# Layer 1's adaLN blocks summed in the scan and the output projection instead of in the MLPs and the q, k projections

## The chip, the cores and the metric

The kernel runs on one core of one Trainium2 chip. The metric is the device time of one execution in microseconds; the time quoted is the median of three executions.

## The reference, cut to what matters

Two layers are applied to 512 latent and 128 context tokens of width 1024. Layer 0 mixes tokens with a bidirectional RWKV-7 scan, layer 1 with neighbourhood attention; each is followed by a squared-ReLU MLP. Each layer has six adaLN vectors (shift, scale and gate, twice), and they depend on the conditioning vectors and on weights alone, not on the tokens:

```python
def ada_mod(cond, w, b):
    m = jax.nn.silu(cond) @ w + b
    return jnp.split(m, 6, axis=-1)

for l in range(DEPTH):            # for the context tokens with c_ctx, for the latent ones with c
    sh1, sc1, gt1, sh2, sc2, gt2 = ada_mod(c, ada_w[l], ada_b[l])
    h = modulate(rms_norm(xs, norm_g[l, 0]), sh1, sc1)
    o = mixer(h, ...)             # l = 0: rwkv7_mixer, l = 1: na_latent / na_context
    xs = xs + gt1[:, None, :] * o
    h = modulate(rms_norm(xs, norm_g[l, 1]), sh2, sc2)
    xs = xs + gt2[:, None, :] * sq_relu_mlp(h, mlp_w1[l], mlp_w2[l])
```

So layer 1's vectors may be made at any time before layer 1 begins, and the later ones up to their use.

## The kernel before, in words

**An adaLN block.** The 6144 columns of one layer's `ada_w` are cut in 24 blocks of 256 columns, 1 MB each. `ada_first` (L279) loads a block as two halves of 512 KB into two buffers of the name `adaraw`, issued on SP, sums it with eight matmuls (16 instructions in the trace) and copies the sum to `adasb` on ACT. `ada_second` (L292) turns the sum over with two small matmuls (4 instructions) and adds the bias on DVE (L300) into `mods`. The pool `adp` has two `adaraw` buffers, so a block's loads wait until the matmuls of the block before have read theirs.

**Where the 48 blocks were summed.** Layer 0's first eight are summed in `start_norm`, its other sixteen in the scan, one a turn. Layer 1's 24 are summed by `ada_later` (L1275), which also takes one block: eight inside MLP 0, twelve inside the q and k projections of `phase_na`, four inside the first quarter of MLP 1.

**The scan.** `phase_scan` (L753) goes through five steps n = 0 to 4, each with four turns e = 0 to 3; (n, e) names a turn. A turn takes one chunk of 32 tokens in either direction: `chain_step` (L981) runs as the generators s0 (direction d = 0) and s1 (d = 1). Each does a state product (`A<-GU,C`), a copy of it on ACT (`Rc`), a solve with the step's inverse (`A<-Rc,TT`), a scaled copy back on ACT (`GU`, L1032), a state update (`B<-GU,C`), and an output product (`A<-GU,C` again). Between these, `fill` (L863) puts the matmuls (`pp<-C,KB`) that prepare the next step, and `invert` (L959) computes the next step's inverse by a long row of small DVE instructions (L973, L976), ending in `TT` (L978). `ada_next` (L777) puts one adaLN block after the first of the turn's fills. The small matmuls of `ada_second` write columns 256 to 259 of the PSUM tile that holds the solve of d = 1, in the same bank. Finished tiles go through `post_half` (L1094), on DVE and GpSimd.

**What sets the order.** While `self.pin` is set, `mm` (L830) chains the scan's matmuls so that TensorE runs them in program order; each other engine has an order laid down when the kernel is built. SP issues nearly all loads, in its own order.

**After the scan.** `wo_first` (L1162) does the output projection for 384 of the 640 tokens. Its weights (L1169) and its inputs `ol` (L1181, L1182) are loaded into the same two `adaraw` buffers, after the last adaLN block. `phase_wo` (L1204) does the other 256 tokens, in eight blocks k with one 512 KB weight block each. Then MLP 0, `phase_na` and MLP 1 follow, whose products are the matmuls of L205.

Of the kernel before, what the change touches and what calls it, by code (L numbers as in the profile page):

```python
# [14 lines left out]
PSUM = bass.MemoryType.PSUM  # L15
# [157 lines left out]
class K:  # L173
# [237 lines left out]
    def rest_begin(self, st):  # L411
        self.sqp = self.pool(st, "sqp", 2)
        self.ada1 = list(range(24))

    def pool(self, st, name, bufs, **k):
        return st.enter_context(self.tc.tile_pool(name=name, bufs=bufs, reuse_waits="tile", **k))
# [336 lines left out]
    def phase_scan(self, st):  # L753
        nc, tc = self.nc, self.tc
        if True:
            pool = lambda name, bufs, **k: self.pool(st, name, bufs, **k)
            self.yp = pool("yp", 4)
            adp = pool("adp", 2)
# [15 lines left out]
            todo, running = [], []  # L774
            ada = [(0, b) for b in range(8, 24)]

# [11 lines left out]
            for n, ts in enumerate(self.steps):  # L788
                for e in range(4):
                    s0, s1 = (self.chain_step(ts, n, e, d) for d in range(2))  # L790
                    next(s0)
                    if pend:
                        for x in pend:
                            next(x)
                        if n == 4 and not self.late:
                            self.late_pools()
                        for t in done.get((n, e - 1) if e else (n - 1, 3), []):
                            todo.append(self.post_half(*t, n == 4 and t[0] % 3))
# [26 lines left out]
            for _ in range(3):  # L825
                for x in todo:
                    next(x)
            self.wo_first(adp)

# [151 lines left out]
    def chain_step(self, ts, n, e, d):  # L981
# [38 lines left out]
        for ph, pp, hp in idx:  # L1020
# [4 lines left out]
                    rhs=Rc[qs, o], start=True, stop=True, tile_position=(32 * q, 32 * q))  # L1025
        if self.ada_sums and d == 1:
            self.ada_second(*self.ada_sums.pop(0), ut[:, 256:260], self.mm)
# [176 lines left out]
    def phase_wo(self):  # L1204

        nc, tc = self.nc, self.tc
        with ExitStack() as st:
            pool = lambda name, bufs, **k: self.pool(st, name, bufs, **k)
            self.wraw = pool("wraw", 4, side="right")
            self.whl = pool("whl", 3, side="right")  # L1210
            self.psl = pool("psl", 4, space=PSUM)
            xp = pool("xp", 8)
# [14 lines left out]
            for k in range(8):  # L1227
# [3 lines left out]
                nc.gpsimd.tensor_copy(self.x[:, k, TS:], xa[:, 256:])  # L1231
                w = self.wblock(self.A["w_o"][k])
                ps = self.psl.tile([P, 512], F32, name="psl")[:, :256]
                for f in range(8):
# [333 lines left out]
```

## Time and profile before

| | |
|---|---|
| median of three executions | 2248.33 us (2247.55 to 2261.33) |
| the profiled execution's own time | 2250.36 us |
| its span, first to last instruction | 2248.5 us |
| TensorE busy | 2007.7 us, 89% |
| VectorE (DVE) busy | 1180.0 us, 52% |
| ScalarE (ACT) busy | 866.0 us, 39% |
| GpSimd (POOL) busy | 463.8 us, 21% |
| scan, by the trace | about 410 to 798 us |
| rest of the output projection | about 798 to 886 us |
| MLP 0, attention layer, MLP 1 | about 886 us to the end |

The shares are means over stages with different limits, so each stage has to be read by itself. Times of the trace count from the span's start. PE is TensorE's matmul, SP the engine that issues most loads. A row in square brackets at a line's end gives the idle time before it and what ended it.

### The profile page before, as it was taken

The page shows a single profiled execution, that of the slowest core. Times are in us where ns is not written, and L with a number is a line of the kernel's source. Part 1 is how long each engine was busy: PE and PEld are TensorE (multiplying, and loading weights), DVE is VectorE, ACT ScalarE, POOL GpSimd, SP SyncE. Part 2 cuts the span into 40 slices and gives each one's busy share as a digit, 9 for nine tenths or more (in the row PEclk, how much of TensorE's full clock was granted, in tenths as well). Part 3 has the DMA queues.
Part 4 walks back from the last instruction along what each step waited for, and adds up shares of the span by engine and source line. Part 5 has one row for each costly group of instructions (what it writes and reads, how often), then busy time and mean ns, then how long its engine had stood idle before and what let it go on. Part 6 is the DMA issues. An engine that isn't in the chain of part 4 may idle for free.

```text
span 2248.5 us, 44838 instructions
## 1 busy us (share of the span) xinstructions
PE 2007.7 (89%) x18516; PEld 1823.6 (81%) x18516; DVE 1180.0 (52%) x2587; ACT 866.0 (39%) x1735; POOL 463.8 (21%) x558
## 2 busy tenths in 40 slices
PE   5898978757665677999999999999999999999999
PEld 3787877646554566999999998888777999999999
DVE  6847667396687766433333334434566643434342
ACT  3544554356553425413131323221576331313130
POOL 0001257566552323101010110000232210101010
PEclk9897989888888798999999999999899999999999
DMA  6454864444443455323232223433311232222221
GB/s 232 123 154 140 251 204 158 141 149 148 131 130 121 101 181 164 94 75 113 76 104 75 94 75 114 137 116 108 111 58 29 75 123 75 75 76 74 74 75 70
DMA packets 161388, 260.01 MB, mean 116 GB/s; under 512 B 46880, under 2 KB 103328, under 8 KB 161184
## 3 DMA queue, kind: packets, MB, share of 16 engines
q1 hardware_dynamic: 146816, 240.37, 34.2%
q10 hardware_dynamic: 14368, 16.78, 2.3%
q8 instruction: 145, 2.38, 0.4%
q14 instruction: 59, 0.48, 0.1%
HBM read 218.18 MB, written 37.35 MB: 114 GB/s over the span
## 4 chain that ended last, share of the span: by engine, by line
PE 73%; DVE 13%; DMA 6%; ACT 3%; POOL 2%; issue 2%; SPq 1%; ACTq 0%; DVEq 0%; POOLq 0%
PE psl L205 53%; PE psl L239 4%; PE ps L1495 2%; DVE invT L973 2%; DVE invX L976 2%; PE po L1532 2%; PE pp L832 2%; POOL C L927 2%; PE pt L1520 2%; DVE C L957 1%; PE psl L286 1%; DMA ld_s<-scr 1%; PE pp L1199 1%; DMA wi<-scr 1%; PE st L548 1%
## 5 line engine op out<-in xcount | busy, mean ns | idle before, releaser
L191 ACT CAST whi<-wraw 128x1024 fp32r<-128x1024 f32 x179 | 187.2, 1048 | 730.9 <-PE psl L205 702.5
L205 PE MATMUL psl<-xh,whi 128*128 128x320 f32 (+1 forms) x1712 | 419.8, 318 | 20.8 <-ACT whi L191 15.1
L205 PE MATMUL psl<-xl,whi 128*128 128x320 f32 (+1 forms) x1712 | 417.0, 316 | 7.9 <-DVE xl L248 7.9
L205 PE MATMUL psl<-xh,wlo 128*128 128x320 f32 (+1 forms) x1712 | 415.0, 315 | 2.6 <-DVE wlo L193 2.6
L205 PEld LDWEIGHTS psl<-xh,whi 128*128 128x128 f32 x1712 | 295.4, 192 | 39.4 <-ACT whi L191 19.3
L205 PEld LDWEIGHTS psl<-xl,whi 128*128 128x128 f32 x1712 | 296.3, 192 | 13.9 <-DVE xl L248 10.0
L205 PEld LDWEIGHTS psl<-xh,wlo 128*128 128x128 f32 x1712 | 297.1, 192 | 5.2 <-DVE wlo L193 3.0
L1152 DVE SCALAR_TENSOR_TENSOR xres<-psl,mods,xres 128x320 f32<-128x320 f32 (+2 forms) x216 | 81.7, 434 | 305.5 <-PE psl L205 305.5
L1315 POOL TENSOR_TENSOR relu<-relu 128x640 f32<-128x640 f32 x64 | 80.8, 1263 | 753.1 <-ACT relu L1314 736.2
L205 PE MATMUL psl<-hhh,wlo 128*128 128x320 f32 x1024 | 233.5, 309 | 0.0
L205 PE MATMUL psl<-hhh,whi 128*128 128x320 f32 x1024 | 233.2, 309 | 0.0
L205 PE MATMUL psl<-hhl,whi 128*128 128x320 f32 x1024 | 233.2, 309 | 0.0
L193 DVE TENSOR_TENSOR wlo<-wraw,whi 128x1024 fp32r<-128x1024 f32 x179 | 222.5, 1245 | 14.2 <-ACT whi L191 14.0
L205 PEld LDWEIGHTS psl<-hhh,whi 128*128 128x128 f32 x1024 | 171.2, 188 | 0.4 <-issue 0.4
L205 PEld LDWEIGHTS psl<-hhl,whi 128*128 128x128 f32 x1024 | 171.1, 188 | 0.0
L205 PEld LDWEIGHTS psl<-hhh,wlo 128*128 128x128 f32 x1024 | 171.1, 188 | 0.0
L1272 DVE TENSOR_TENSOR relu<-psl,rms_b 128x320 f32<-128x320 f32 x128 | 60.7, 486 | 144.4 <-PE psl L205 143.3
L832 PE MATMUL pp<-C,KB 128*64 128x128 f32 x1280 | 97.6, 298 | 27.2 <-DVE C L957 13.1
L248 DVE TENSOR_TENSOR hhl<-relu,hhh 128x640 fp32r<-128x640 f32 x64 | 53.4, 834 | 127.9 <-ACT hhh L247 127.8
L832 PEld LDWEIGHTS pp<-C,KB 128*64 128x64 f32 x1280 | 79.9, 149 | 41.3 <-issue 20.7
L957 DVE TENSOR_TENSOR C<-pp,cstsb 64x512 f32<-64x512 f32 x80 | 55.1, 689 | 76.5 <-ACT C L954 68.9
L1032 ACT ACTIVATE GU<-A 32x256 f32<-32x256 f32 x160 | 60.0, 375 | 84.3 <-DVE mods L300 51.8
(288 smaller groups left out, 3389.7 us busy)
## 6 DMA issues: line engine op xcount, KB each, us to landing
wraw<-in_mlp_w SPq DMA_DIRECT2D x128, 512.0 KB, 3.5
adaraw<-in_ada_w SPq DMA_DIRECT2D x96, 512.0 KB, 4.9
ld_d<-scr SPq DMA_DIRECT2D x20, 512.0 KB, 4.1
ld_s<-scr SPq DMA_DIRECT2D x20, 512.0 KB, 3.9
bias<-in_bias SPq DMA_DIRECT2D x16, 384.0 KB, 3.5
scr<-ta SPq DMA_DIRECT2D x16, 325.0 KB, 3.5
wi<-scr SPq DMA_DIRECT2D x20, 260.0 KB, 4.5
scr<-bp SPq DMA_DIRECT2D x16, 320.0 KB, 4.6
```

Source lines behind the costliest of these rows:

```text
L191: nc.scalar.copy(hi, raw)
L193: nc.vector.tensor_tensor(lo, raw, hi.bitcast(F32), op=ALU.subtract)
L205: self.nc.tensor.matmul(ps[g][:, :e - c], lhsT=a[:, k, :], rhs=b[:, c:e], start=(k == 0 and j == 0), stop=(k == n - 1 and j == 2))
L239: nc.tensor.matmul(ps, lhsT=a[:, tc_], rhs=w, start=(k == 0 and j == 0), stop=(k == KT - 1 and j == 2))
L248: (lo_eng or nc.vector).tensor_tensor(xl, src, xh.bitcast(F32), op=ALU.subtract)
L832: r = (op or self.nc.tensor.matmul)(*a, **k)
L927: nc.gpsimd.tensor_tensor(rev(o) if s == 0 else o, v4(sh, s, ww)[hs], f[hs], op=ALU.mult)
L957: nc.vector.tensor_tensor(C[o, 8 * h:8 * h + 8, :], pn[o, :, 0:64], mask[o], op=ALU.mult)
L1032: nc.scalar.activation(gu[64 - 64 * hp:96 - 64 * hp, hp, pp].rearrange("p b v -> p (b v)"), U[32 * q:32 * q + 32, :], AF.Copy, scale=-0.5)
L1152: nc.vector.scalar_tensor_tensor(out[:, a:b], ps[g][:, o:o + b - a], gate[:, k, j:j + 1], x[:, a:b], op0=ALU.mult, op1=ALU.add)
L1272: nc.vector.tensor_tensor(t[:, c], ps[q][:, :HALF], rb[:, c], op=ALU.mult)
L1315: nc.gpsimd.tensor_tensor(t, t, t, op=ALU.mult)
```

## The change

The list of layer 1's blocks is made at the start of the scan and appended to the scan's own list, so that this list has 40 blocks. A second block is taken in each turn of step 0, and in the turns e = 0, 2 and 3 of the later steps; it stands right after the first state product of d = 0. `ada_second` is done in either direction's solve tile, no longer in that of d = 1 alone. The scan's 36 places take 16 blocks of layer 0 and 20 of layer 1; `phase_wo` gets a pool `adp` of its own and a fifth PSUM buffer, and sums the last four blocks in its first four turns k. The calls of `ada_later` in the MLPs and in the projections find the list empty and do nothing.

```diff
     def rest_begin(self, st):
         self.sqp = self.pool(st, "sqp", 2)
-        self.ada1 = list(range(24))
...
     def phase_scan(self, st):
         nc, tc = self.nc, self.tc
+        self.ada1 = list(range(24))
...
-            ada = [(0, b) for b in range(8, 24)]
+            ada = [(0, b) for b in range(8, 24)] + [(1, b) for b in self.ada1]
...
                     next(s0)
+                    if n == 0 or e != 1:
+                        ada_next()
                     if pend:
...
                 for x in todo:
                     next(x)
+            self.ada1 = [b for _, b in ada]
             self.wo_first(adp)
...
-        if self.ada_sums and d == 1:
+        if self.ada_sums:
             self.ada_second(*self.ada_sums.pop(0), ut[:, 256:260], self.mm)
...
-            self.psl = pool("psl", 4, space=PSUM)
+            self.psl = pool("psl", 5, space=PSUM)
+            self.adp = pool("adp", 2)
...
                 w = self.wblock(self.A["w_o"][k])
+                self.ada_later()
```

## Rows read from the trace of the kernel before

**Rows 1.** The page's busy times: us, share of the span, instructions.
```profile
PE 2007.7 (89%) x18516; PEld 1823.6 (81%) x18516; DVE 1180.0 (52%) x2587; ACT 866.0 (39%) x1735; POOL 463.8 (21%) x558
```

**Rows 2.** Chain of waits in MLP 0 and the k projection: start, us, engine, tile, line.
```profile
1023.85 1.00 PE psl L286 x16
1029.18 0.34 PE psl L296 x4
...
1395.24 0.54 PE psl L296 x4
...
1399.83 1.00 PE psl L286 x16
```

**Rows 3.** Busy time by stage: window, length, engines, clock, DMA share, GB/s.
```profile
454.00:508.00 54.00, 26.51 (x708) 21.38 (x699) 52.94 (x141) 26.83 (x66) 31.88 (x47) 0.78 0.47 145
508.00:536.00 28.00, 26.35 (x692) 20.73 (x692) 9.65 (x22) 18.95 (x51) 15.48 (x22) 0.94 0.44 139
...
737.00:770.00 33.00, 21.48 (x679) 18.11 (x670) 28.43 (x73) 12.84 (x31) 3.37 (x3) 0.81 0.45 111
...
798.00:843.00 45.00, 34.10 (x211) 31.88 (x209) 31.50 (x66) 10.08 (x12) 8.01 (x5) 0.96 0.66 201
843.00:890.00 47.00, 32.03 (x207) 30.64 (x208) 32.69 (x49) 28.26 (x63) 18.68 (x22) 0.82 0.51 160
...
1024.00:1130.00 106.00, 106.00 (x742) 104.70 (x735) 39.07 (x69) 28.06 (x38) 8.79 (x7) 1.00 0.28 92
```

**Rows 4.** Waits in the scan: who waited for whom, us in total, times, longest.
```profile
ACT GU L1032 <- DVE mods L300: 51.8, 16, 13.0
...
SPq L284 <- PE pp L832: 45.7, 16, 13.5
```

**Rows 5.** Timeline of PE, DVE and ACT at the end of turn (3, 3).
```profile
719.72 0.61 PE L832 MATMUL A<-cstsb,adasb 128*128 128x2 f32 x4
...
731.40 0.15 DVE L300 TENSOR_TENSOR mods<-A,parsb 128x4 f32<-128x4 f32 x1
...
731.59 1.57 ACT L1032 ACTIVATE GU<-A 32x256 f32<-32x256 f32 x4 [13.02 <-DVE mods L300]
```

**Rows 6.** Timeline of PE in turns (0, 0) and (0, 1).
```profile
415.68 2.73 PE L832 MATMUL pp<-C,KB 128*64 128x128 f32 x16 [3.14 <-POOL C L927]
...
443.14 1.08 PE L832 MATMUL A<-GU,C 128*32 128x64 f32 x32 [8.60 <-ACT Y L1049]
```

**Rows 7.** Chain of waits from the scan to MLP 0: transfers and projection.
```profile
411.86 6.35 DMA adaraw<-in_ada_w
...
525.90 4.73 DMA adaraw<-in_ada_w
...
784.87 3.70 DMA adaraw<-scr
...
791.47 4.05 PE pp L1199 x14
...
879.29 4.97 DMA wraw<-in_mlp_w
```

**Rows 8.** Timeline of PE: the solve that opens a step, and turn (2, 3).
```profile
507.95 1.08 PE L832 MATMUL A<-Rc,TT 32*32 32x64 f32 x32 [19.16 <-DVE rsq_t L262]
...
644.91 1.10 PE L832 MATMUL A<-GU,C 128*32 128x64 f32 x64
...
648.33 1.07 PE L832 MATMUL pp<-adaraw,condp 128*32 128x256 f32 x16
...
736.71 1.07 PE L832 MATMUL A<-Rc,TT 32*32 32x64 f32 x32 [1.32 <-DVE TT L978]
```

**Rows 9.** Loads and casts that reuse adaraw: SP's timeline, then instructions (min/median/max ns).
```profile
719.93 0.41 SPq L1169 DMA_DIRECT2D adaraw<-in_w_o  x1
...
L1171 ACT CAST ww<-adaraw x8: 1034/1046/1047, 734.0 to 831.5; 128x1024 fp32r<-128x1024 f32 x8
L1172 DVE TENSOR_TENSOR ww<-adaraw,ww x8: 1210/1216/1226, 740.2 to 832.6; 128x1024 fp32r<-128x1024 f32 x8
```

## The prediction

> **What bounds the kernel now.** I read the page's busy times first: TensorE is busy for 89% of the span and nothing else for more than 52% [rows 1]. That share is a mean, so I went to the busy time by stage next, and there the kernel falls in two [rows 3]. In MLP 0 TensorE is busy for all 106.00 us of a stretch of 106 us, at the full clock. Before that, no stage is like it. The scan swaps its limit twice in a step: while a step's inverse is computed, VectorE is busy for 52.94 us of 54 and TensorE for 26.51; in the two turns that follow, TensorE has 26.35 of 28 and VectorE 9.65 [rows 3]. In the scan's last step VectorE leads with 28.43 of 33 us, and in the rest of the output projection the two share the time [rows 3].
>
> Last I read the chain of waits and the waits themselves. In the MLPs and projections an adaLN block stands in the chain as a piece of its own, with matmuls on both sides [rows 2]: whatever is taken out there shortens the kernel. In the scan the reader is to see two waits that adaLN blocks make already [rows 4]: ACT's `GU` copy of d = 1 waits for the bias addition `mods` on VectorE, sixteen times in sixteen blocks, 51.8 us together and up to 13.0; and SP stands before block loads for 45.7 us until matmuls have read the two `adaraw` buffers.
>
> **What is removed.** A block costs 1.00 + 0.34 = 1.34 us in an MLP and 1.00 + 0.54 = 1.54 us in the projections [rows 2]. Twelve blocks are in MLPs and twelve in projections: 12 x 1.34 + 12 x 1.54 = 34.6 us. TensorE has no idle time there to refill, so this is a saving in full; bounds 32 (all at 1.34) and 36 (the same, and some 10% for restarting the product around them).
>
> **What is added, stage by stage.** Twenty of the blocks go to the scan and four to the projection. On TensorE alone they cost 24 x (1.07 + 0.61), about 40 us, the instructions' times in the scan [rows 5, 8]; the question is how much of this, and of the waits that come with it, lies under other work.
>
> *Step 0.* In turn (0, 0) the first block stands right after the first product, and its load takes 6.35 us from 411.86 [rows 7]; TensorE's fixed order holds the solve behind it until about 418.3. The second block can be loaded only when the first has been read, so it ends near 425 and not 419: 6 us late. But the next turn has 8.60 us in which TensorE waits for ACT, which waits for loads [rows 6], and that takes up the 6 us and most of the 2 us that a second block costs there. I take 2.5 us for this and for loads that share the queue; bounds 0 and 8 (6 + 2, cover gone).
>
> *Turns e = 0 of steps 1 to 3.* The new block stands between the first product and the solve, where TensorE waits for the inverse, 19.16 us in step 1 [rows 8]: free. Its two small matmuls come after the solve, where TensorE is the limit: 0.61 us warm, about 1.0 at the lower clock, three times, is 2 to 3 us. Turns e = 1 get no new block. I take 3; bounds 2 and 6 (the 1.07 us shows too in the steps where the wait for the inverse is short, as the 1.32 us of step 4 [rows 8]).
>
> *Turns e = 2 and 3 of steps 1 to 3.* Here VectorE is the limit. Twelve additions of 0.15 us [rows 5] are 2 us for it, of which six are new, 1 us. TensorE may be late, and this is where: the second block of a turn cannot end before the first has been read (1.07 us), its second half reloaded (4.73 [rows 7]) and summed (0.5), about 6.4 us after the first began. In turn (2, 3) the first product ends near 645.5 and the block begins at 648.33 [rows 8]; with the new pieces ahead of it, it would end at about 5.0 us after that product, so TensorE stands still for some 1.4 us. Behind it wait the second half of the fill and the product of d = 1. VectorE has a backlog in these turns, so I take 3 us for all six; bounds 0 and 9 (six times 1.5).
>
> *Step 4 and the first projection.* Seven blocks come where there were none. Each brings a wait of a `GU` copy for VectorE, on the mean 51.8 / 16 = 3.2 us [rows 4], and in (3, 3) it was 13.02 us, because the addition was queued behind other VectorE work: the matmuls ended near 720.3 and the addition ran at 731.40 [rows 5]. All seven in the open would be 23 us. But the pace of step 4 is set by VectorE, busy for 86% [rows 3], so most of each wait passes while VectorE does work that is needed anyway: I take 4. Then the buffers: the projection's first weights are now requested at 719.93 [rows 9], some 55 us ahead. After the change they can be requested only after the last block of (4, 3), near 785. Transfer, cast and subtraction take 4.7 + 1.05 + 1.22 = 7 us [rows 7, 9] before the same buffer can take an input tile, and the inputs then come two at a time, where now the last of them lands at 788.6 and TensorE starts in earnest at 791.47 [rows 7]. I reckon about 10 us more until the first block of the product ends. Of this the rest of the projection can win back half, since TensorE is busy for 34.10 of 45 us there [rows 3]: 5. Together 9; bounds 3 and 20.
>
> *The second projection.* Four blocks of 1.34 us are 5.4, in a stage where TensorE has 15 idle us of 47, of which 5 are the wait for the first MLP weights after its own last product [rows 3, 7] and can't cover it. I take 3; bounds 0 and 6.
>
> The sum: 2250.4 - 34.6 + 2.5 + 3 + 3 + 9 + 3 = 2236.3 us. It is made against the profiled execution's own 2250.36 us, which is 2 us above the median; that difference is below what I can resolve. With all bounds at one end it is 2250.4 - 36 + 5 = 2219, at the other 2250.4 - 32 + 49 = 2267.
>
> One rule speaks against the change. Of the wait in [rows 5] the Trainium skill says why it is there: its page "PSUM — Partial Sum Buffer", section "Terms", has it that no two engines may be in one bank of one partition at the same time, two reads included, and that the compiler keeps such accesses apart. The trace agrees: all sixteen copies waited for the addition that read the same bank. By that rule the solve tile of d = 0, which only ACT reads now, gets the same wait.
>
> **The rivals.**
>
> *All of it is hidden.* TensorE is idle for half of every inverse stage and VectorE for two thirds of the turns between [rows 3]; if step 4 also swallows its blocks, only the bounds below remain: about 2219 us. Against it stand the buffers, which no idle engine helps.
>
> *The two `adaraw` buffers starve the chain.* If loads take longer than 4.73 us as the scan moves 20 MB more, and the 1.4 us of (2, 3) shows in each of the eleven turns with two blocks and no long wait between (three of step 0, eight later), with the 6 us of (0, 0): 11 x 1.4 + 6 = 21, of which my sum has about 4: 2253 us. For it: SP's 45.7 us before these loads already [rows 4]. Against it: the load for a turn's first block has half a turn's time.
>
> *The wait for VectorE takes the place of the work removed.* Twenty more copies (sixteen of d = 0, four of d = 1 in step 4) wait 3.2 us each [rows 4]: 65 us, if all stand in the chain. With the other terms (13 without the 4 of step 4's waits, rounded down as they overlap) 2250.4 - 34.6 + 65 + 13 = 2294 us, and 2261 with half of it exposed. It decides from (34.6 - 13) / 20, about 1.1 us, left open per wait; slower by over 1% from about 2.2 us. For it: the 13.02 us [rows 5]. Against it: in the turns where TensorE is the limit VectorE is idle two thirds of the time, so there a wait is short, and between the solve and the update that needs the copy lie 3 us of other matmuls.
>
> *The change does nothing*, because something else fills the freed time: 2270 or so, with what was added. TensorE's 106.00 of 106 us [rows 3] all but excludes it.
>
> **How the numbers follow.** Chances: the sum 0.40, between 2226 and 2248; all hidden 0.30; starved buffers 0.14; waits for VectorE 0.14; no effect 0.02. The prediction is the first: 2236 us. About 1% (22 us) is what a measurement of this kernel can tell from no change. Faster by over 1% is all hidden, 0.30. Slower by over 1% (above 2271) is the part of the third rival with over 2.2 us a wait, 0.09. The rest, 0.61, is within 1%. The range goes from 2216, just under the lower bound, to 2262, the third rival half exposed; above lies about 0.12, below 0.06. The likeliest case by itself spans 2226 to 2248.
>
> **What would show it.** Right: MLP and projection stages shorter by 34 us with no L286 in them; the inverse stages as long as before with VectorE full; the stage from 737 to 843 longer by about 9, with TensorE waiting for L1184 or L1171 when the projection begins. Wrong: turns (n, 2) and (n, 3) longer, with TensorE waiting for `adaraw` (starved buffers), or `GU` copies of d = 0 waiting for L300 by several us and TensorE's `B<-GU,C` after them (VectorE). If neither is there and the scan is not longer at all, all of it was hidden.

## The result and the profile after

The changed kernel takes 2269.35 us (median of twelve executions, 2259.84 to 2275.0) and the kernel before 2251.57 us beside it: a ratio of 1.0073, 95% interval 1.0052 to 1.0093. The change costs 16 us or so, where I had forecast a gain of 14, and the time lies above the upper end of my range, 2262. Single executions of x9 and x18 took more than twice the usual time, the profiled one of x18 among them, so there is no trace to read x18 from.

TensorE's busy time and share answer to [rows 1]. They hide the loss: the share is the same 89%, of a longer span.

```profile
PE 2027.1 (89%) x18516; PEld 1837.7 (81%) x18516; DVE 1178.9 (52%) x2587; ACT 867.4 (38%) x1735; POOL 455.5 (20%) x558
```

To see where it went I cut both spans at events that both kernels have: the scan's first state product, the first solve of each step, the last state product, the last product of `wo_first` (L1202 now), the first product of MLP 0, the end.

| stage | before, us | after, us | difference |
|---|---|---|---|
| scan, step 0 | 97.2 | 102.7 | +5.5 |
| step 1 | 84.2 | 85.2 | +1.0 |
| step 2 | 71.7 | 90.5 | +18.8 |
| step 3 | 72.8 | 69.0 | -3.8 |
| step 4 | 62.1 | 78.5 | +16.4 |
| first projection | 43.0 | 60.6 | +17.6 |
| second projection | 44.6 | 50.8 | +6.2 |
| MLP 0 to the end | 1362.1 | 1318.9 | -43.2 |

So 43.2 us came back from MLP 0 on and 61.7 were spent for it before; the profiled spans differ by 18.7. How far such a reading can be trusted is shown by four kernels with the same scan (before, x1, x8 and x12 below): in one execution of each it took 388.1 to 390.6 us. The next rows, busy time by stage of the kernel after (window, length, then busy time and count of PE, PEld, DVE, ACT and POOL, granted clock, DMA share, GB/s), are those of steps 2 and 4 and the first projection.

```profile
599.00:689.00 90.00, 61.62 (x1420) 47.94 (x1412) 54.74 (x144) 45.95 (x121) 45.25 (x69) 0.79 0.51 163
...
758.00:837.00 79.00, 44.66 (x1101) 33.91 (x1089) 50.45 (x125) 30.12 (x66) 21.99 (x19) 0.75 0.61 165
837.00:897.00 60.00, 43.09 (x199) 37.71 (x200) 33.19 (x59) 10.39 (x15) 13.15 (x13) 0.78 0.60 180
```

No engine is busy all the time in any of them. The whole scan, from its first to its last state product, in the same columns, first before and then after:

```profile
410.70:798.80 388.10, 248.60 (x6346) 200.74 (x6345) 272.29 (x728) 193.05 (x490) 190.91 (x252) 0.82 0.45 134
```
```profile
410.90:836.80 425.90, 296.61 (x6722) 228.74 (x6721) 272.37 (x751) 198.88 (x506) 178.87 (x245) 0.79 0.54 167
```

TensorE has 48.0 us more of work and the scan is 37.8 us longer: TensorE's idle time fell from 139.5 to 129.3 us, by 10 only. VectorE's busy time is the same to 0.1 us. The idle time that was there before hardly served as cover. The costliest groups of PE in those two stretches (line, tile, shape, count, busy, mean ns, idle just before) say where the work went, first before and then after:

```profile
L832 PE MATMUL pp<-adaraw,condp 128*32 128x256 f32 x256 | 20.9, 453 | 1.6 <-issue 1.1 <-DVE C L957 0.2
L832 PE MATMUL A<-cstsb,adasb 128*128 128x2 f32 x64 | 10.1, 263 | 0.0
```
```profile
L835 PE MATMUL pp<-adaraw,condp 128*32 128x256 f32 x576 | 56.5, 505 | 39.5 <-DMA adaraw<-in_ada_w 31.1 <-DVE C L960 4.4 <-DVE Y L1050 1.9
L835 PE MATMUL A<-cstsb,adasb 128*128 128x2 f32 x144 | 26.0, 285 | 0.7 <-ACT adasb L289 0.7
```

The blocks' sums have 35.6 us more of busy time and 31.1 us of a wait that did not exist: TensorE stands before a block whose load has not landed, 18 times. The waits of the scan after that answer to [rows 4] (who for whom, us in total, times, longest):

```profile
ACT GU L1035 <- DVE mods L300: 108.7, 33, 8.4
...
SPq L284 <- PE pp L835: 71.2, 40, 6.8
...
SPq L284 <- DMA adaraw<-in_ada_w: 27.2, 11, 5.0
```

Both have about doubled, from 51.8 to 108.7 us and, the two rows of SP together, from 45.7 to 98.4. How a turn suffers is to be read from the timeline of PE and ACT in turn (1, 2) and of PE in (2, 0) and (2, 1) (start, us, engine, line, operation, in brackets the idle time before it and its releaser):

```profile
547.90 1.93 PE L835 MATMUL pp<-adaraw,condp 128*32 128x256 f32 x16 [4.42 <-DVE C L960]
...
565.58 0.64 ACT L900 ACTIVATE w<-wi 128x520 f32<-128x520 f32 x1 [6.17 <-DVE wi L899]
...
568.95 1.08 PE L835 MATMUL A<-Rc,TT 32*32 32x64 f32 x32 [6.51 <-ACT Rc L1018]
...
586.94 1.96 DVE L981 STREAM_TRANSPOSE TT<-invX 128x1024 f32<-128x1024 f32 x1
...
598.82 0.65 PE L835 MATMUL A<-Rc,TT 32*32 32x64 f32 x32 [0.43 <-ACT Rc L1018]
...
604.85 1.08 PE L835 MATMUL pp<-adaraw,condp 128*32 128x256 f32 x8 [3.82 <-DMA adaraw<-in_ada_w]
...
622.59 1.08 PE L835 MATMUL A<-Rc,TT 32*32 32x64 f32 x32 [5.45 <-ACT Rc L1018]
```

In (1, 2) the new block stands 4.42 us before a tile of `pp` that VectorE has yet to read; later the solve waits 6.51 us for `Rc`, because ACT's fixed order has an exponential ahead of that copy, and the exponential waits 6.17 us for VectorE. By these steps the solve of (2, 0) comes at 598.82, ten us after its inverse is ready at 588.9. Before, TensorE had waited 12.99 us for that inverse:

```profile
592.15 1.08 PE L832 MATMUL A<-Rc,TT 32*32 32x64 f32 x32 [12.99 <-DVE TT L978]
```

Step 1 looks free (+1.0 us) because this wait paid for it. Step 2 has nothing left to pay with. Its turn (2, 0), counted from its first solve to that of (2, 1), takes 23.8 us, before 14.8. At the end of the step TensorE waits again, for an inverse that itself comes late: it is ready 90.3 us after the step's first solve, before 71.6.

```profile
689.31 1.08 PE L835 MATMUL A<-Rc,TT 32*32 32x64 f32 x32 [6.17 <-DVE TT L981]
```

### The profile page after: what moved, and what is told of

It is laid out like the page before. It is cut to its first block, busy times and chain, and to the rows that moved or that the text cites. A ratio compares the mean times of both kernels' runs of the same rounds, so it can differ in the third digit from the quotient of the medians.

```text
span 2267.2 us, 44814 instructions
## 1 busy us (share of the span) xinstructions
PE 2027.1 (89%) x18516; PEld 1837.7 (81%) x18516; DVE 1178.9 (52%) x2587; ACT 867.4 (38%) x1735; POOL 455.5 (20%) x558
## 4 chain that ended last, share of the span: by engine, by line
PE 58%; DMA 1%; DVE 1%; ACT 1%; issue 0%; ACTq 0%; DVEq 0%; SPq 0%
PE psl L205 47%; PE psl L239 3%; PE ps L1500 2%; PE po L1537 2%; PE pt L1525 1%; PE pp L1202 1%; DMA ol<-scr 0%; PE pk L677 0%; DVE xl L1262 0%; DMA bias<-in_bias 0%; DMA xi<-in_xT 0%; DMA adaraw<-in_ada_w 0%; ACT whi L191 0%; DVE wlo L193 0%; ACT xh L1261 0%
## 5 line engine op out<-in xcount | busy, mean ns | idle before, releaser
L205 PE MATMUL psl<-xh,whi 128*128 128x320 f32 (+1 forms) x1712 | 415.0, 316 | 17.5 <-ACT whi L191 11.8
L205 PEld LDWEIGHTS psl<-xl,whi 128*128 128x128 f32 x1712 | 294.6, 192 | 16.0 <-DVE xl L248 10.1
L193 DVE TENSOR_TENSOR wlo<-wraw,whi 128x1024 fp32r<-128x1024 f32 x179 | 220.5, 1233 | 14.3 <-ACT whi L191 13.9
L248 DVE TENSOR_TENSOR hhl<-relu,hhh 128x640 fp32r<-128x640 f32 x64 | 53.4, 834 | 127.9 <-ACT hhh L247 127.7
L835 PE MATMUL pp<-C,KB 128*64 128x128 f32 x1280 | 102.6, 311 | 14.3 <-POOL C L930 7.5
L835 PEld LDWEIGHTS pp<-C,KB 128*64 128x64 f32 x1280 | 84.9, 157 | 29.3 <-issue 16.4
L1035 ACT ACTIVATE GU<-A 32x256 f32<-32x256 f32 x160 | 59.9, 374 | 114.7 <-DVE mods L300 108.7
L960 DVE TENSOR_TENSOR C<-pp,cstsb 64x512 f32<-64x512 f32 x80 | 55.1, 689 | 85.2 <-ACT C L957 77.9
```

The costliest lines, as they stand in the source:

```text
L193: nc.vector.tensor_tensor(lo, raw, hi.bitcast(F32), op=ALU.subtract)
L205: self.nc.tensor.matmul(ps[g][:, :e - c], lhsT=a[:, k, :], rhs=b[:, c:e], start=(k == 0 and j == 0), stop=(k == n - 1 and j == 2))
L248: (lo_eng or nc.vector).tensor_tensor(xl, src, xh.bitcast(F32), op=ALU.subtract)
L835: r = (op or self.nc.tensor.matmul)(*a, **k)
L960: nc.vector.tensor_tensor(C[o, 8 * h:8 * h + 8, :], pn[o, :, 0:64], mask[o], op=ALU.mult)
L1035: nc.scalar.activation(gu[64 - 64 * hp:96 - 64 * hp, hp, pp].rearrange("p b v -> p (b v)"), U[32 * q:32 * q + 32, :], AF.Copy, scale=-0.5)
```

## The experiments

A ratio is to the kernel before, run on the same chip; the kernels ran on several chips, on which the kernel before took 2248.1 to 2251.6 us, so ratios compare better than times. "Scan" is the time from the first to the last state product; where a kernel's blocks lie elsewhere, the blocks that remain behind the scan are the last of the list's order, so the four places in MLP 1 are emptied first. (The expectations for x8, x12 and x15 to x17 name MLP 0 as the giver; by the stages it was MLP 1.)

### What the removed work was worth, and the four blocks in the second projection

**x1**, the kernel before without layer 1's blocks:

```diff
-        self.ada1 = list(range(24))
+        self.ada1 = []
+        self.nc.vector.memset(self.mods[1], 0.0)
```

> The kernel before with layer 1's 24 adaLN blocks left out altogether (layer 1's shifts, scales and gates are zero, so its part of the result is not computed). It prices the removal by itself. The prediction's sum says 34.6 us less than the kernel before (bounds 32 and 36), about 2217. The two traces say more: from the first product of MLP 0 to the end the kernel before takes 2248.5 - 886.4 = 1362.1 us and the changed one 2267.2 - 948.2 = 1319.0, so 43 us less, about 2208. If the saving is as first priced, the rest of the 43 us is something else that the change brought to the later stages.

Measured: 2207.23 us, ratio 0.9803 (0.9767 to 0.9839), so 24 blocks are worth 44 us (36 to 52), as the two traces had said. Scan and projections are within 2 us of the kernel before.

**x8**, the kernel before with four blocks in the second projection (`phase_wo` as in the change, `if k < 4`):

```diff
+            self.psl = pool("psl", 5, space=PSUM)
+            self.adp = pool("adp", 2)
...
+                if k < 4:
+                    self.ada_later()
```

> The kernel before, with four of layer 1's blocks moved from MLP 0 to the output projection's second part, nothing in the scan. The MLP gives 4 x 1.83 = 7.3 us (44 us for 24 blocks, measured) or 4 x 2.7 = 11 if the first blocks cost more there, and the stage between the first projection's last product and MLP 0 grows: by the 3 us of the forecast, 2244 to 2248; by the 6.2 us that it grew in the changed kernel, 2246 to 2251. If the growth is 6 us or more, these four blocks are worth nothing where they went.

Measured: 2252.28 us, 1.0006 (0.9987 to 1.0024). MLP 1 is 381.1 us from its first to its last hidden tile, against 387.7: four blocks gone, 1.65 us each. The second projection took 53.6 us against 44.6, more than either growth that I had named. Nothing is gained by these four.

### The waits for VectorE

**x3**, the additions of both blocks in the solve tile of d = 1:

```diff
-        if self.ada_sums:
-            self.ada_second(*self.ada_sums.pop(0), ut[:, 256:260], self.mm)
+        for j in range(len(self.ada_sums) if d == 1 else 0):
+            self.ada_second(*self.ada_sums.pop(0), ut[:, 256 + 4 * j:260 + 4 * j], self.mm)
```

> The changed kernel with both bias additions of a turn put into the solve tile of d = 1; the tile of d = 0 is read by ACT alone again. Theory 2: the 17 or so new waits of d = 0 (108.7 us in 33 waits against 51.8 in 16) go, and with them some 15 to 25 us: about 2250. Theory 1: the buffers stay as they are, so within 5 us of the changed kernel, 2264 to 2274.

Measured: 2276.19 us, 1.0129 (1.0087 to 1.0171). The `GU` copies' wait for the addition fell from 108.7 to 62.4 us, and the kernel became no faster: by the medians it is 7 us slower than the changed one, and the intervals of the two ratios overlap. Both theories had forecast less. TensorE's wait for block loads rose from 31.1 to 57.4 us.

**x5**, the additions on ACT, which makes the copies itself (36 blocks), and **x7**, the same in the kernel before (16 blocks):

```diff
+        if mm:
+            for i in range(2):
+                nc.scalar.activation(m[:, i, :], pm[:, 2 * i:2 * i + 2], AF.Identity, bias=ab[:, i:i + 1])
+            return
```

> The changed kernel, with the bias addition of the scan's adaLN blocks (36 of them) as two small additions on ACT instead of one on VectorE, so that no GU copy waits for another engine's read of its bank. In the changed kernel GU copies wait 108.7 us for the addition in 33 places between 405 and 830 us, before 51.8 in 16. Theory 'wait for VectorE': most of the scan's 41 us (steps 2 and 4 above all) is this wait; without it 2235 to 2250. Theory 'buffers and loads': the two adaraw buffers set it, ACT has some 0.2 us more per addition: 2265 to 2275. Theory 'more work in a fixed order': the copies come earlier but TensorE's order is as full as before: 2260 to 2270, with the time between steps hardly changed.

> The kernel before, with the bias addition of the scan's 16 blocks on ACT. Theory 'wait for VectorE': the 51.8 us of waits go, the turns of steps 1 to 3 shorten by some 1 us each: 2235 to 2245. The other theories: VectorE's inverse sets the pace of those steps and the waits were hidden, 2248 to 2254.

Measured: x5 2272.01 us, 1.0097 (1.0076 to 1.0118); x7 2257.3 us, 1.0025 (1.0007 to 1.0043). In x5 no copy waits for VectorE's addition, the scan is 8 us shorter (417.7), and that is not seen in the whole; in its trace the first projection is 3.9 us longer and attention, where nothing was changed, 7.1. ACT pays with 72 small instructions. In x7, where 32 of them take the place of 16 waits, the kernel loses some 6 us, above what either theory had forecast. So in the changed kernel the waits may be worth a few us; they are not the main cause.

### Loads and sums

**x2**, no blocks in step 4; seven go back to the MLP, `phase_wo` keeps four:

```diff
-                    if n == 0 or e != 1:
+                    if n == 0 or n < 4 and e != 1:
...
-                    ada_next()
+                    if n < 4:
+                        ada_next()
```

> The changed kernel without any block in step 4 of the scan; the seven blocks that stood there go back to MLP 0, the projection keeps its four. Traces: from step 4's first solve to the end of the first projection the changed kernel takes 139 us (758.3 to 897.4) and the one before 105 (736.7 to 841.8). Theory 1 (two adaraw buffers: the projection's weights can't be asked for before the last block, and second blocks wait for their load): most of the 34 us comes back, less 7 x 1.34 = 9.4 for the blocks in MLP 0, so 2269 - 34 + 9 = about 2245, with the first weight request again some 50 us ahead. Theory 2 (copies wait for the bias addition in the same PSUM bank): about half of it, step 4's own 16 us, comes back, and the projection stays long: about 2262.

Measured: 2258.75 us, 1.0025 (1.0 to 1.005). The first projection is back at 39.8 us. The scan is 415.4 us, still 27 longer than before, with thirteen new blocks in it. The time lies between the two theories, 2245 and 2262.

**x4**, the first block of each turn without its load; **x6**, the seven blocks of step 4 without load; **x9**, all twenty without (each sums the constant `lnwb` instead):

```diff
+            if load:
                 raw = pool.tile([P, 4, 256], F32, name="adaraw")
                 nc.sync.dma_start(raw, self.A["ada_w"][l, blk, :, 4 * h:4 * h + 4])
...
-rhs=raw[:, c, :],
+rhs=raw[:, c, :] if load else self.lnwb[:, c % 2, :],
```

> The changed kernel, where each added block (the one right after the first product of d = 0) sums a tile that lies in SBUF already, without loads of its own, so that these blocks' values are not the adaLN sums; the matmuls, the copies, the bias additions and their waits stay, and 16 of the scan's 36 MB of block loads go. Theory 1: the stalls of second blocks (TensorE waits for adaraw 31 us in the scan) go, and the scan's steps 0 to 3 and step 4's turns win 15 to 25 us; the projection's weights still come late: about 2249. Theory 2: the waits for the additions stay, so within 6 us of the changed kernel.

> The changed kernel, where the seven blocks in step 4 load nothing and sum over the constant tile lnwb instead (so their seven columns of mods are wrong); all else stands. Theory 'buffers and loads': the first projection's weights are requested near 745 us again and not at 824, its 60.6 us go back to 43 to 46, and the kernel takes 2250 to 2256. Theory 'wait for VectorE': step 4's 78.5 us stay above 74, as the additions still stand before the GU copies. Theory 'more work in a fixed order': projection and step 4 stay within 4 us of the changed kernel, 2263 to 2270.

> The changed kernel, where all twenty blocks that the change put into the scan load nothing and sum over the constant tile lnwb (their columns of mods are wrong); the four in the projection's second part load as before. Without the loads of the sixteen first blocks the kernel took 14 us less, without those of step 4 19 us less. Theory 'buffers and loads' (all of the cost over what the MLPs gave back is loads): the two add up, 2233 to 2240, and the scan's TensorE waits for adaraw (31 us in the changed kernel) are gone. Theory 'TensorE's own work' (the blocks' matmuls stand in a chain with no cover left): what the loads cost is taken up by other waits in part, 2242 to 2252.

**x10**, x9 without second halves; **x11**, all loads, but a quarter of the sums and no second halves:

```diff
+            for c in range(1 if new else 4):      # x11; x10: range(4)
...
+        if new:
+            return None                           # no adasb, no ada_second
```

> As the last, and the twenty blocks in the scan also have no second half: no copy of adasb, no two small matmuls behind the solve, no bias addition before the GU copy (their columns of mods are zero). What is left of them is 640 matmuls of 128x256 in the scan, 320 of them new, which took 35.6 us more of TensorE in the changed kernel. Theory 'TensorE's own work': the 80 small matmuls of 0.285 us go, some 16 to 23 us with their share of a lower clock, so 14 to 20 us less than the last kernel. Theory 'buffers and loads': 0 to 5 us less. Theory 'wait for VectorE' (108.7 us of GU copies before the addition): 25 us less or more.

> The changed kernel, where the twenty blocks in the scan keep their loads, but only the first of each load's four column groups is summed, and there is no second half (their columns of mods are zero): loads and buffers without most of TensorE's work. A kernel without layer 1's blocks in the scan and with the four in the projection would be near 2215 (2207 without any, and some 8 for those four). Theory 'buffers and loads': 30 us or so stay, 2243 to 2255. Theory 'TensorE's own work': loads cost only because the sums are behind them and late; 2222 to 2235.

**x13**, new loads of a quarter of the bytes; **x14**, new loads issued by GpSimd:

```diff
+            if new:
+                nc.sync.dma_start(raw[:, 0], w[:, 0])                     # x13
...
+            (nc.gpsimd if new else nc.sync).dma_start(raw, ...)           # x14
```

> The changed kernel, where each half load of the twenty blocks put into the scan brings 128 KB and not 512 KB, into the same two buffers and in the same place of SP's queue; the four sums read that one piece (their columns of mods are wrong). Without these loads the kernel took 2242. Theory 'bytes' (20 MB more share the transfer engines with the scan's other loads): nearly all of the 27 us come back, 2242 to 2248. Theory 'two buffers and one queue' (a load is requested when the sums before it are done and then takes its latency, 5.2 us at 512 KB, 2.2 us at 128 KB): half comes back, 2250 to 2260.

> The changed kernel, with the loads of the twenty blocks put into the scan issued from GpSimd's queue and not SP's. SP stands before adaLN loads for 98 us in the changed kernel (71.2 for sums, 27.2 for an earlier load), 45.7 before, with GU, pbuf and wi loads queued behind. Theory 'one queue' (what stands behind these loads is late): 2245 to 2258. Theory 'two buffers': the same waits for adaraw on TensorE, 2262 to 2275, and more if GpSimd's own work is held up by the waits for buffers.

Measured (ratios with intervals; the request is SP's first issue of the projection's weights, L1169 in [rows 9]; TensorE's time is that of the scan):

| kernel | us | ratio | scan | TensorE busy, idle | weights requested | first projection |
|---|---|---|---|---|---|---|
| before | 2251.57 | 1 | 388.1 | 248.6, 139.5 | 719.93 | 43.0 |
| after | 2269.35 | 1.0073 (1.0052-1.0093) | 425.9 | 296.6, 129.3 | 824.41 | 60.6 |
| x2 no step 4 | 2258.75 | 1.0025 (1.0-1.005) | 415.4 | 292.9, 122.5 | 741.97 | 39.8 |
| x4 first ones without load | 2254.94 | 1.0034 (1.0-1.0068) | 405.8 | 284.5, 121.3 | 799.45 | 63.1 |
| x6 step 4 without load | 2250.68 | 1.0001 (0.998-1.0022) | 415.3 | 294.6, 120.7 | 730.01 | 48.8 |
| x9 no new load | 2242.24 | 0.9963 (0.9944-0.9982) | 412.1 | 290.4, 121.7 | 719.34 | 48.3 |
| x10 first halves only | 2232.58 | 0.9924 (0.9894-0.9953) | 402.1 | 270.6, 131.5 | 718.56 | 48.0 |
| x11 loads, quarter sums | 2276.77 | 1.0126 (1.0097-1.0155) | 416.5 | 274.3, 142.2 | 826.61 | 69.1 |
| x13 quarter loads | 2259.53 | 1.0046 (1.0014-1.0077) | 409.8 | 293.1, 116.7 | 803.78 | 65.6 |
| x14 GpSimd's queue | 2280.31 | 1.0155 (1.0126-1.0185) | 422.2 | 296.2, 126.0 | 816.93 | 61.8 |

The rows behind the table for x9, x10, x11 and x13, one fence each (busy time in the scan, columns as above):

```profile
405.80:817.90 412.10, 290.36 (x6745) 232.85 (x6744) 276.50 (x750) 202.07 (x512) 186.48 (x252) 0.80 0.42 127
```
```profile
407.80:809.90 402.10, 270.55 (x6665) 214.57 (x6664) 280.03 (x728) 196.12 (x492) 190.69 (x252) 0.82 0.43 130
```
```profile
416.80:833.30 416.50, 274.25 (x6401) 208.23 (x6400) 265.06 (x726) 188.56 (x480) 181.82 (x244) 0.81 0.55 169
```
```profile
404.00:813.80 409.80, 293.07 (x6721) 224.58 (x6720) 267.87 (x750) 198.10 (x504) 177.61 (x244) 0.80 0.44 135
```

Read from x10 over x9 to the changed kernel, the scan's 37.8 us come apart: first halves alone make it 14.0 longer (388.1 to 402.1), second halves 10.0 more (412.1), loads 13.8 more (425.9). Other orders of taking away would give other shares, since x11, with loads and little work, already has 416.5; the parts share their waits. What is firm: without any load the scan is still 24 us longer, so the loads are not all of it, and with loads and a quarter of the sums it is 28 us longer, so the work is not all of it either. x11 is slower than the changed kernel, although it does less: its scan is 9.4 us shorter, but its first projection is 8.5 longer and its scan began 6 later (below).

The first projection is simpler. SP's request for its first weights, in the timeline of after, x13 and x9:

```profile
824.41 1.72 SPq L1172 DMA_DIRECT2D adaraw<-in_w_o  x2
```
```profile
803.78 0.80 SPq L1176 DMA_DIRECT2D adaraw<-in_w_o  x2
```
```profile
719.34 0.83 SPq L1176 DMA_DIRECT2D adaraw<-in_w_o  x2
```

Where a block of step 4 loads into the two buffers, the weights are requested at 799 us or later and the projection takes 60 us and more; where none does, they are requested before 742 and it takes 40 to 49. In all seven kernels with such loads (the five of the table, x3 and x5) 69 to 77 us pass from the request to the projection's last product; in x3 the scan itself ended so late that only 51.6 of them lie behind it. Small loads don't help there (x13): it is not the bytes but that the buffers are taken. In the scan they do help: x13's 409.8 us are near those of x9, with no load, although TensorE's wait for `adaraw` is 50.8 us there. So the loads cost twice: about 12 us behind the scan by holding the buffers, about 14 within it, and there, by one execution each, by their size. That they stand in SP's queue is not shown to cost anything: x14 put them in another, the scan stayed within 4 us, and GpSimd then waited for the same buffers. It became slower as a whole, so what SP's queue costs by itself is not told apart from what GpSimd's own work lost:

```profile
POOL adaraw L284 <- PE pp L835: 82.9, 22, 12.9
```

What lengthens step 4 is not its own blocks alone. Of the 16.4 us, 14.7 lie in turn (4, 1). From its first solve to that of (4, 2) it takes 11.3 to 14.3 us in the kernel before and the seven made from it that have such a trace, and 17.6 to 26.7 in the changed one and the ten made from that: 26.0 after, 24.5 in x2 with no block in step 4, 26.7 in x10 with neither new loads nor new second halves. There TensorE, in its fixed order, stands before the transposes of a finished output tile (`post_half`). First before, then after, where ACT's part of the finishing waits for the store of an earlier tile, then x2:

```profile
758.70 0.63 PE L832 MATMUL pp<-cstsb,Y 128*128 128x128 f32 x4 [2.69 <-DVE pbuf L1140]
```
```profile
783.93 0.63 ACT L1123 ACTIVATE pbuf<-Y 128x512 f32<-128x512 f32 x1 [5.84 <-DMA scr<-pbuf]
...
795.44 1.09 PE L835 MATMUL pp<-cstsb,Y 128*128 128x128 f32 x4 [7.59 <-DVE Y L1134]
```
```profile
795.84 1.09 PE L836 MATMUL pp<-cstsb,Y 128*128 128x128 f32 x4 [9.26 <-DVE Y L1135]
```

Why the finishing comes so late in these kernels no run settles. In x6, without loads in step 4, that step still takes 75.1 us, as the theory of the wait for VectorE had it, while the time (2250.68) is at the edge of what buffers and loads had forecast.

Of the other expectations here, x4 came nearer to the stalls (2249) than to the additions. x9 lies at the edge of 'TensorE's own work' (2242). x10 took 9.7 us less than x9, between the theories. x11 lies above both. x13 falls where 'two buffers and one queue' had it, and x14 above 2275, where its expectation had put a GpSimd that is held up.

### Where a block costs nothing

**x12**, six blocks behind layer 0's first eight:

```diff
+        for b in range(6):
+            ps = ps2.tile([P, 512], F32, name="adp")
+            self.ada_second(*self.ada_first(1, b, adp, ps[:, :256]), ps[:, 256:260])
```

> The kernel before, with six of layer 1's blocks right behind the eight of layer 0 at the very start, and not in MLP 0; nothing else moves. Between 44 and 60 us TensorE is busy for 4.5 of 16 us there, the transfers stand at 0.05 to 0.50, and VectorE sets the pace with 16 of 16. If a block is free where transfers and TensorE both stand idle, MLP 0's 2.3 to 2.8 us for each is kept: 2234 to 2242. If the first weights of the projections wait behind these loads or for their buffers, the start grows by the 12 loads (some 1.6 us each, 19 us) and the kernel takes 2252 to 2258.

Measured: 2270.47 us, 1.0102 (1.0062 to 1.0141). The scan begins at 422.1 us, 11 later. Two rows, busy time from 44 to 60 us, first before and then x12:

```profile
44.00:52.00 8.00, 1.16 (x2) 0.44 (x2) 8.00 (x15) 5.13 (x9) 0.00 (x0) 1.00 0.50 129
52.00:60.00 8.00, 3.32 (x10) 2.52 (x11) 8.00 (x13) 2.58 (x4) 0.00 (x0) 1.00 0.05 12
```
```profile
44.00:52.00 8.00, 6.79 (x53) 2.92 (x52) 6.86 (x16) 1.56 (x5) 0.00 (x0) 0.61 1.02 415
52.00:60.00 8.00, 6.84 (x40) 3.93 (x38) 1.83 (x5) 1.21 (x3) 0.00 (x0) 0.50 0.57 163
```

VectorE, the limit there, was busy all 16 us and now stands idle for 6 of the last 8: its order has the blocks' additions among its own work, and they wait for TensorE (three waits of 1.93, 2.65 and 2.41 us for L296), which does the sums one after another at a granted clock of 0.50 to 0.61 and itself waits for loads for under 1 us. The first product of the projections starts at 62.21 us, before at 52.23. TensorE and the transfers had been idle there, and still the place was not free. The time lies above both forecasts. The trace is of an execution of 2257.49 us, so the other 13 us up to the median are not in these rows.

**x15, x16, x17**, the kernel before with three, five or seven blocks directly ahead of the solve that opens a step, where TensorE waits 19.16 us [rows 8], 12.99 us and, in x16, 12.56 us for the inverse; both halves are summed there, in a tile of `pp`, so no `GU` copy waits for them. **x18** is the same edit with five blocks in turns without that wait:

```diff
                     k = self.fill(f[0])
+                    for _ in range(PLAN.get((n, e), 0)):
+                        pt = self.pp_tile()
+                        a = self.ada_first(*early.pop(0), adp, pt[:, :256], self.mm)
+                        self.ada_second(*a, pt[:, 512:516], self.mm)
                     next(s0)
+# x15 {(1,0): 2, (2,0): 1}   x16 {(1,0): 3, (2,0): 2}   x17 {(1,0): 3, (2,0): 2, (3,0): 2}
+# x18 {(1,2): 1, (1,3): 1, (2,2): 1, (2,3): 1, (3,2): 1}
```

> The kernel before, with three of layer 1's blocks where TensorE waits for a step's inverse and nothing else stands behind: two right before the solve of turn (1, 0), where it waits 19.2 us, one before that of (2, 0), 13.0 us. Their second halves are summed there too, in the block's own tile of pp, so that no GU copy waits for them. MLP 0 is rid of three blocks at 1.83 to 2.8 us each. Theory 'cover is where TensorE waits for VectorE's inverse': nothing is added, 2243 to 2247. Theory 'one queue': the six loads stand in SP's queue before the loads of the next turns and cost as much: 2250 to 2257.

> As the last with three blocks in (1, 0) and two in (2, 0). A further block needs a buffer read, 5 us of load and 1.5 us of sums, so three end some 15 us after the first begins, and two some 8. Theory 'cover': 5 x 1.83 to 2.8 saved, 2237 to 2243. Theory 'one queue' or 'two buffers': the later loads come late and hold the solve or the loads behind them, 2250 to 2260.

> The kernel with five blocks under the inverse (2240), and two more before the solve of (3, 0), where TensorE waits 12.6 us for the inverse in that kernel's profile. Two blocks end some 8 to 9 us after the first begins, so the solve is not held. Theory 'cover': MLP 0 is rid of two more, 4 to 5 us: 2234 to 2238, and the time from the scan's first product to the end of the state products stays at 384 us (+-2). Theory 'one queue' or 'two buffers': 2240 to 2250 and a longer scan.

> The same edit as with five blocks under the inverse, the same number of blocks and loads, the same tiles, but one each before the solve of the turns (1, 2), (1, 3), (2, 2), (2, 3) and (3, 2), where TensorE doesn't wait for the inverse and the turn's other block follows close behind. Theory 'place' (a block is free only where its load and its sums both lie under a wait that does not depend on them): 10 to 20 us more than with the five under the inverse, 2250 to 2260. Theory 'number' (each block costs its TensorE time and its load wherever it is): 2238 to 2244 as there.

| kernel | us | ratio | scan |
|---|---|---|---|
| x15, three | 2253.1 | 1.0009 (0.9978 to 1.004) | 385.4 |
| x16, five | 2240.0 | 0.9974 (0.9957 to 0.9992) | 384.4 |
| x17, seven | 2250.13 | 1.0009 (0.9987 to 1.003) | 393.7 |
| x18, five elsewhere | 2263.33 | 1.0066 (1.0043 to 1.009) | not known |

x16 is faster than both kernels: by 0.3% against before, with the upper end of its interval just under 1, and, by the two ratios, 1.0% against after. Its scan is 3.7 us shorter than before with five blocks more, and MLP 1 is 6.6 us shorter. The timeline of PE before the solve of (1, 0) in x16, with the end of the inverse on DVE:

```profile
486.94 1.05 PE L837 MATMUL pp<-adaraw,condp 128*32 128x256 f32 x16
...
495.15 1.08 PE L837 MATMUL pp<-adaraw,condp 128*32 128x256 f32 x8 [3.78 <-DMA adaraw<-in_ada_w]
...
500.81 1.08 PE L837 MATMUL pp<-adaraw,condp 128*32 128x256 f32 x8 [1.84 <-DVE invT L978]
503.28 1.08 PE L837 MATMUL pp<-adaraw,condp 128*32 128x256 f32 x8 [1.39 <-DMA adaraw<-in_ada_w]
503.39 1.92 DVE L983 STREAM_TRANSPOSE TT<-invX 128x1024 f32<-128x1024 f32 x1
...
505.85 1.07 PE L837 MATMUL A<-Rc,TT 32*32 32x64 f32 x32
```

Here TensorE waits for loads and for tiles as in the changed kernel, and it costs about half a us, since the inverse, for which the solve behind them has to wait, is ready only at 505.31. The same five blocks in full turns (x18) cost 23 us more: the place makes the difference, not the number. That the wait for the inverse is what makes the place good is argued from x16's trace, as x18 has none beside it.

Against it stand x15 and x17. Neither is told from before, and their times lie where, or at the edge of where, the rival theories ('one queue', 'two buffers') had put them. In x15's trace the scan is as short as x16's, but it began 5 us later than before (below). In x17 the two blocks in (3, 0) gained nothing, and the scan is 9 us longer than x16's; of these, 7 lie in steps in which both kernels have the same blocks. Whether that is the two blocks or something else stays open, and so the gain itself rests on x16 alone.

## Why the prediction was wrong, point by point

In sum, the added terms were 20.5 us and came to 61.7, and the saving was 34.6 and came to 43.2. My own bounds reached up to 2267, beyond the range's 2262, and the measured time lies above both. I had put what a measurement can tell from no change at 1%; the interval of this one reaches 0.2% to either side.

*The saving* was sized too low: 34.6 us forecast (32 to 36), 43.2 in the profiles, of which 2.5 lie in attention, where nothing was changed. By stage, MLP 0 gave 12.9, the q and k projections 21.2, MLP 1 6.6: about 1.7 us a block, where I had taken 1.34 and 1.54 from a block's own matmuls [rows 2]. The 10% that I allowed for restarting the product around a block came from no row; the 40.7 us without attention are some 18% above 34.6. x1 agrees (44).

*Step 0*: 2.5 forecast, +5.5, within its bounds.

*Turns of steps 1 to 3*: 3 + 3 forecast, 15 at the bounds; measured +1.0, +18.8, -3.8, so +16. The mechanisms I named are there: in (2, 0) the turn's second block waits 3.82 us for its load, and in (2, 1), which has one block only, the solve waits 5.45 us for `Rc`. The failing step is that I counted the late block alone, 1.4 us a turn, and let each turn begin on time. Delays add up until a wait for the inverse absorbs them, and that wait was 13 us in step 2, and no more than 1.32 us in step 4 [rows 8]. I had called it free for a block at e = 0 and had not asked what else would draw on it.

*Step 4 and the first projection*: 9 forecast, 3 to 20 allowed; measured 16.4 + 17.6 = 34.0. This is the largest miss, 25 of the 41 us by which the added terms were too small. The mechanism of the projection was right (the two buffers, x6 and x9 show it), but the request came at 824.41 and not near 785, and half of it was not won back. In step 4 I argued that VectorE, at 86% [rows 3], paced the stage anyway and would hide the waits of the `GU` copies; it was busy for 50.45 us of the 79 after. What I had left out is the finishing of output tiles in TensorE's order: turn (4, 1) grew by 14.7 us, 7.59 of them in one wait for it, and in x2 it grew by 13.2 with no block in step 4. So the seven blocks' own waits, which I had priced, are not what lengthened the step; why the finishing is late stays open.

*The second projection*: 3 forecast, +6.2, at its upper bound; x8 shows four blocks worth nothing there.

*The rivals.* "All hidden" is gone: even without loads the twenty blocks lengthen the scan by 24 us. "The two buffers starve the chain" named a resource that counts, as the new loads are worth 27 us (x9), but at 2253 us it was too low by 16: it left out that the projection behind needs the same buffers, and that the blocks lengthen the scan by 24 us without any load. "The wait for VectorE" forecast 3.2 us a wait and there are 33 of 3.3, 17 more than before; but to take them away (x5) does not make the kernel faster, and all second halves together, waits and matmuls, are worth 10 us (x9 against x10). So a wait that repeats in every turn need not be the one that costs. By the Trainium skill's page "PSUM — Partial Sum Buffer", section "Terms", two engines must not be in one bank at once, reads included, and I had concluded that the copies of d = 0 would get this wait. The trace agrees: of the 33 places 14 are copies of d = 0, of the 16 before none was. At 4.0 us each they are the one sign of being wrong that I had named; of the other, (1, 2) and (2, 3) are longer by 6.8 and 9.3 us, but TensorE's longest wait for `adaraw`, 3.82 us, stands in (2, 0).

*What the sum shares with the rival "all hidden"* was wrong: that TensorE's idle half of an inverse stage is cover. Of its 139.5 us of idle time in the scan the change used 10, and x16, with five blocks under the inverse, 21 (384.4 us, 266.1 of them busy). Much of the rest lies, as the rows of (1, 2) to (2, 1) show, between dependent instructions of a fixed order, and a block put there delays what follows it.
The Trainium skill's page "Perfetto Trace Analysis", section "Engine Utilization", has the reading that I passed over: where the use of both the matmul engine and memory is low, a kernel is bound by latency, that is by stalls and dependencies. The trace fits it for step 2 of the kernel after, with TensorE at 61.62 of 90 us, VectorE at 54.74 and a DMA share of 0.51.

## What to carry to other kernels

Of an engine's idle time ask what ends it, and whether the moved work can delay that. Where it ended in the wait for the inverse, five blocks cost nothing that can be seen (x16); the same five elsewhere cost 23 us, and 48.0 us of work put into all of the scan made it 37.8 us longer. It is no guarantee, as three and seven blocks under the same waits gained nothing. Count such a wait once, however many places draw on it. And of work moved with its loads ask who next needs the buffers: here that cost 12 us in the stage behind.

## What the runs showed of the hardware

Kernels with the same instructions ahead of the scan began it up to 12 us apart (x13 at 404.0 us, x2 at 416.2). Busy time from 40 to 160 us, before and x15:

```profile
40.00:80.00 40.00, 22.92 (x84) 18.35 (x84) 37.45 (x56) 21.14 (x32) 0.00 (x0) 0.84 0.37 105
80.00:160.00 80.00, 80.00 (x496) 66.06 (x495) 41.94 (x75) 35.50 (x63) 0.00 (x0) 0.99 0.43 135
```
```profile
40.00:80.00 40.00, 21.22 (x78) 17.10 (x78) 38.10 (x54) 21.20 (x33) 0.00 (x0) 0.61 0.35 105
80.00:160.00 80.00, 80.00 (x452) 65.66 (x451) 35.48 (x66) 30.75 (x56) 0.00 (x0) 0.87 0.40 123
```

In a stretch in which TensorE is idle for almost half of the time its mean granted clock was 0.84 in one execution and 0.61 in another; in the second it was thus at 1.2 and not 2.4 GHz for most of the stretch. In the full stretch behind it the clock was 0.99 or 0.87, and 496 or 452 matmuls ran in 80 us. Attention, unchanged too, took 127.7 to 136.7 us from its first to its last product of scores. So an effect of 5 us in this kernel can be read from the scan, which agrees to 2.5 us between kernels in which it is the same, and not from a span.
